# A third quarter of x turned by VectorE's blocks, where TensorE transposed it before

## The chip, the core and the metric

The kernel runs on one core of one Trainium2 chip. The time is the device time of one execution in microseconds (us); of several runs the median is given. The engines are TensorE (PE in the profile, PEld its weight loads), VectorE (DVE), ScalarE (ACT), GpSimd (POOL) and SyncE (SP, here the queue that issues most DMAs).

## What is computed

One step of a decoder layer for 256 prompt tokens and 8 x 4 sample tokens, 288 in all, with 2048 features, in float32. Only the first lines matter here: the residual x meets one wide input projection, and everything else follows from that.

```python
def hybrid_layer(x, ..., w_in, ...):
    proj = x @ w_in
    split_points = np.cumsum(SPLITS)[:-1].tolist()
    gB, gC, h, q, k, v, z, b_logit, a_logit, m_a, m_b = jnp.split(proj, split_points, axis=-1)
...
    merged = jax.nn.sigmoid(m_a) * y_a + jax.nn.sigmoid(m_b) * y_b
    x = layer_norm(ALPHA * x + merged @ w_o, ln1_g, ln1_b)
    hid = jnp.square(jax.nn.relu(x @ w_up))
    x = layer_norm(ALPHA * x + hid @ w_down, ln2_g, ln2_b)
```

## The kernel before

The whole kernel is a list of some 500 *blocks* (512 KB of weights each) that TensorE works through in order, one `matmuls(i)` after the other. For float32 accuracy each weight tile `raw` is split into a rounded part `hi` (ScalarE, `split_hi`, line 187) and a rest `lo = raw - hi` (VectorE, `split_lo`, through `tt`, line 142); the activations are split the same way into `xh` and `xl`. A block is 24 matmuls of 288 columns in four groups of six: twice xh and xl against hi (line 219), then twice xh against lo (line 221). The 288 columns are 256 prompt tokens and 32 sample tokens, so the first xl matmul of a block needs both.

The features of x must lie on the partitions: x has to be turned. This is done at the start, beside the first blocks, by quarters of 512 features (4 of the 16 tiles in `xh` and `xl`). The order of the blocks is set by hand: blocks 0 to 3 are wide ones, which use the first two quarters (0 and 1 the first, 2 and 3 the second), blocks 4 and 5 use quarter 2, blocks 6 and 7 quarter 3. All engines run their instructions in the order in which the code issues them; nothing reorders them.

There are two ways to turn a quarter.

- By TensorE (quarters 0, 1 and 2): `x_steps` gives eight transposes of 128x128 into PSUM (line 957), ScalarE casts the result to `xh` (line 963), VectorE subtracts it to get `xl` (line 142). These steps are put between the matmuls of the block before by the list `fill`: after the second pair of lo matmuls one step is taken from it. For quarter 2 this is `x_fill(2)`, put in at `i == 3`.
- By VectorE (quarter 3 alone): `x_turn` turns 32x32 blocks in one instruction, `xr[3]` to `xtb` (line 980); `x_moves` then moves sixteen pieces of 32 partitions by 256 columns to their places in `xm` (line 987), ten on GpSimd and six on ScalarE; `x_last` casts `xm` to `xh` on ScalarE (line 992) and subtracts on VectorE, in two halves.

The sample's 32 columns of each quarter are always transposed by TensorE (`x_sample`, line 941), cast by ScalarE (line 946) and subtracted by VectorE. The loop that sets the order around the change, in the kernel before:

```python
matmuls(i)
if i == 4:
    x_last()
if i < 6:
    for u, step in {0: ((1, 2),), 1: ((2, 1), (3, KB))}.get(i, ((i + 2, KB),)):
        split_hi(u, step)
        split_lo(u, step)
if i == 2:
    x_turn()
    x_moves(gps.tensor_copy, range(10))
if i == 3:
    x_moves(act.copy, range(10, 16))
```

In the program's names `hi`, `lo` and `raw` carry running numbers: before, `lo_262` is block 2's, `lo_269` block 3's, `lo_299` block 4's, `lo_358` block 5's, `lo_398` block 6's; with the change these are `lo_264`, `lo_280`, `lo_310`, `lo_367`, `lo_403`.

Of the kernel before, what the change touches and what calls it, by code (L numbers as in the profile page):

```python
# [9 lines left out]
F32 = mybir.dt.float32  # L10
# [6 lines left out]
P = 128  # L17
# [88 lines left out]
def hybrid_kernel(ctx: ExitStack, tc: tile.TileContext, A):  # L106
# [3 lines left out]
    def pool(name, bufs=1, **kw):  # L110
        return ctx.enter_context(tc.tile_pool(name=name, bufs=bufs, **kw))
# [10 lines left out]
    def nm(s):  # L122
        counter[0] += 1
        return f"{s}{counter[0]}"

    def gtile():
        n = nm("g")
        return gp.tile([P, 512], F32, tag="g", name=n)
# [9 lines left out]
    act, dve, pe, gps, sp = nc.scalar, nc.vector, nc.tensor, nc.gpsimd, nc.sync  # L138


    def tt(out, a, b, op):
        dve.tensor_tensor(out=out, in0=a, in1=b, op=op)  # L142
# [18 lines left out]
    fill = []  # L161

    def at(i, f):
        due.setdefault(i, []).append(f)
# [18 lines left out]
    def split_hi(i, step=KB):  # L183
        if i < len(blocks):
            his[i] = wp.tile([P, KB, GW], F32R, tag="hi", name=nm("hi"))
            for k in range(0, KB, step):
                act.copy(his[i][:, k:k + step], raw[i][:, k:k + step])  # L187

    def split_lo(i, step=KB):
        if i < len(blocks):  # L190
            los[i] = wp.tile([P, KB, GW], F32R, tag="lo", name=nm("lo"))
            r = raw[i] if blocks[i][0].get("by_token") else raw.pop(i)
            for k in range(0, KB, step):
                tt(los[i][:, k:k + step], r[:, k:k + step], his[i][:, k:k + step], SUB)
# [682 lines left out]
    tx = tx_cm.__enter__()  # L877
# [9 lines left out]
    xr = [tx.tile([P, 2, 512], F32, name=f"xr{i}") for i in range(4)]  # L887
# [1 line left out]
    xpr = A["x_prompt"][0].rearrange("(b p) f -> p b f", p=P)  # L889
    xsr = A["x_sample"].rearrange("b t (c j p) -> c (b t) j p", j=4, p=P)  # L890

    xtb, xm = (tx.tile([P, 1024], F32, name=n) for n in ("xtb", "xm"))
    hwr = tx.tile([112, 768], F32, name="hwr")
    har = tx.tile([76, 256], F32, name="har")
    lnr = tx.tile([33, P], F32, name="lnr")
# [43 lines left out]
    def x_sample(i):  # L939
        g = gtile()  # L940
        pe.transpose(g[:, 0:P], xs4[:, i * P:(i + 1) * P], ident)
        gv = g[:, 0:P].rearrange("p (t j) -> p j t", j=4)
        xv, xw = (u[:, 4 * i:4 * i + 4, NP_:NT] for u in (xh, xl))

        def out(copy=act.copy):
            copy(xv, gv)  # L946
            tt(xw, gv, xv, SUB)
        return out
# [21 lines left out]
    def x_fill(i):  # L970
        def step(u):
            def f():
                turns, out = x_steps(i)[u]()
                for g in turns + out:
                    g()
            return f
        return step(0), lambda: x_sample(i)(), step(1)

    def x_turn():
        dve.transpose(out=xtb, in_=xr[3].rearrange("p b c -> p (b c)"))  # L980

    def x_moves(copy, ns):
        src = xtb.rearrange("p (b k j r) -> p j b k r", b=2, k=4, j=4)
        dst = xm.rearrange("p (k b w r) -> p w b k r", k=4, b=2, w=4)
        for n in ns:
            w, j = n // 4, n % 4
            copy(dst[32 * j:32 * j + 32, w], src[32 * w:32 * w + 32, j])

    def x_last():
        for k in (0, 2):  # L990
            ks, xv = slice(12 + k, 14 + k), xm.rearrange("p (k t) -> p k t", k=4)[:, k:k + 2]
            act.copy(xh[:, ks, 0:NP_], xv)
            tt(xl[:, ks, 0:NP_], xv, xh[:, ks, 0:NP_], SUB)

# [577 lines left out]
    def states_out(t0, t1, npr, n, tag, prompt, sample):  # L1572
        st = gd["pool"].tile([P, t1 - t0, 32], F32, tag=tag, name=nm("st"))
        for t in range(t0, t1, 8):
            dve.transpose(out=st[:, t - t0:t - t0 + 8].rearrange("p t c -> p (t c)"),
                          in_=stBA[:, t:t + 8].rearrange("p t c -> p (t c)"))
        for i in range(4):
            for dst, r0, r1 in ((prompt, 0, npr), (sample.rearrange("b j c -> (b j) c"), npr, n)):
                gps.dma_start(dst.rearrange("r (t i c) -> i r t c", i=4, c=32)[i], st[32 * i + r0:32 * i + r1])
# [18 lines left out]
    t, h0, l0 = raw.pop(0), his[0], los[0]  # L1598
# [21 lines left out]
    idle = lambda: None  # L1620
# [23 lines left out]
    for i in range(len(blocks)):  # L1644
        cur[0] = i
        ahead = AHEAD if i > 9 else 2
        if i == 10:
            split_hi(i + 2)
            split_lo(i + 2)
        if i > 5:  # L1650
            split_hi(i + ahead)
        if i in (1, 3):
            a_, s_, b_ = x_fill(i // 2 + 1)
            fill.extend([idle, a_, s_, b_])
        if i == 5:
            fill.extend([idle, idle, lambda: x_sample(3)()])
        if i == 6:
            fill.extend([idle, idle, idle, idle, hist_tiles, hist_tiles2])
        if i == 7:
            tx_cm.__exit__(None, None, None)  # L1660
            gcm = tc.tile_pool(name="gdn", bufs=1)
            gpool = gcm.__enter__()
            gd["pool"] = gpool
            gd["w1"] = [gpool.tile([P, 640], F32, tag=f"w1{u}", name=f"w1{u}") for u in range(2)]
            for w in gd["w1"]:
                gps.memset(w[:, 0:3], 0.0)
            gps.memset(stBA, 0.0)
            for G in range(2):
                gd["kq", G] = gpool.tile([P, 4, 4, 2, 64], F32, tag="kq", name=f"kq{G}", bufs=2)
                gd["kqs", G] = gpool.tile([P, 2, 4, 8, 4], F32, tag="kqs", name=f"kqs{G}", bufs=2)  # L1670
                gd["v", G] = gpool.tile([P, 2, 4, 2, 64], F32, tag="vf", name=f"vf{G}")
                gd["vs", G] = gpool.tile([P, 4, 8, 4], F32, tag="vfs", name=f"vfs{G}")
        if i > 7 and sgen:
            if i == mark["merge"]:
                for _ in sgen:
                    pass
                sgen = None
            else:
                next(sgen, None)
                if aux and next(aux[0], aux) is aux:  # L1680
                    aux.pop(0)
            if i == mark["z"] + 4:
                states_out(24, 32, 2, 18, "vf", A["new_conv_a_prompt"][0, 0], A["new_conv_a_sample"][0])
            if i == mark["conv"] + 1:
                gd["ao"] = ap_.tile([P, 2, H, NT], F32, tag="ao", name="ao")
        late = i >= mark["end"] - 1
        if i > 5 and not late:
            split_lo(i + ahead)
        for f in due.pop(i, ()):
            f()  # L1690
        if late:
            split_lo(i + ahead)
        if i == mark["merge"]:
            gcm.__exit__(None, None, None)
            p3 = pool("p3")
            ph["pool"] = p3
            r1 = p3.tile([P, KT, NT], F32R, tag="R1", name="ahl")
            r4 = p3.tile([P, KT, NX], F32R, tag="R4", name="ohl")
            ph["mg"] = p3.tile([P, KT, NX], F32, tag="R3", name="mg")[:, :, 0:NT]

            def halves(key, r, src):
                for q in range(2):
                    s = slice(4 * q, 4 * q + 4)
                    s8 = slice(8 + 4 * q, 12 + 4 * q)
                    act.copy(r[:, s, 0:NT], src[:, s, :])
                    tt(r[:, s8, 0:NT], src[:, s, :], r[:, s, 0:NT], SUB)
                ph[key + "h"], ph[key + "l"] = r[:, 0:8, :], r[:, 8:16, :]

            halves("a", r1, gd["ao"][:, 0])
            at(i + 9, lambda: halves("o", r4, gd["ao"][:, 1]))  # L1710
        if i == mark["down3"]:
            tail_tiles()
        if i == mark["down3"] - 60:
            tail_consts()
        if i == mark["end"] - 3:
            sample_sum()
        if i == mark["end"] - 1:
            sample_products()
        matmuls(i)
        if i == 4:  # L1720
            x_last()
        if i < 6:
            for u, step in {0: ((1, 2),), 1: ((2, 1), (3, KB))}.get(i, ((i + 2, KB),)):
                split_hi(u, step)
                split_lo(u, step)
        if i == 2:
            x_turn()
            x_moves(gps.tensor_copy, range(10))
        if i == 3:
            x_moves(act.copy, range(10, 16))  # L1730
        if i == 10:
            load(i + 6)
        load(i + ahead + 4)
        if 4 <= i < 8:
            rest[i - 4]()
# [33 lines left out]
```

## Time and profile before

| | us |
|---|---|
| median of 3 runs | 1661.09 (1659.30 to 1661.68) |
| the profiled execution | 1658.95 |
| its span, first to last instruction | 1656.8 |
| busy in the span: TensorE | 1648.6 |
| VectorE | 981.2 |
| ScalarE | 785.8 |
| GpSimd | 138.8 |

The profile is one execution; its times run from the span's start. Between span and time lie 2.15 us. Matmuls are pipelined: one of 288 columns lasts 0.29 us from start to end, and the next begins 0.13 us after it. So the starts are what to read, not the busy time. In a row, the name left of the arrow is written and those right of it are read, buffer numbers are left out (`lo<-raw,hi`), x and a number at the end count the instructions in the row, and what stands in brackets is idle time before the row and what ended it.

### The profile page before, as it was taken

The numbers are of one execution on the slowest core, as the hardware profiler recorded it, in microseconds if no ns is written. First come the engines' busy times: TensorE is split into PE (matmuls) and PEld (weight loads), VectorE is DVE, ScalarE is ACT, GpSimd is POOL, SyncE is SP. The second block draws the span as 40 slices with busy tenths as digits, with TensorE's granted clock in tenths as the row PEclk, the third lists the DMA queues.
The fourth block names the chain that finished last, engine by engine and source line by source line (L and its number), as shares of the span: only waits on it lengthen the run. The fifth ranks groups of instructions, "written<-read, shape, count | busy, mean of one in ns | idle before, by whom it ended". The sixth has DMA issues, their size and how long they took to land.

```text
span 1656.8 us, 31402 instructions
## 1 busy us (share of the span) xinstructions
PE 1648.6 (100%) x13130; PEld 1634.0 (99%) x13130; DVE 981.2 (59%) x1299; ACT 785.8 (47%) x1231; POOL 138.8 (8%) x273
## 2 busy tenths in 40 slices
PE   9999999999999999999999999999999999999998
PEld 8999999999999999999999999999999999999997
DVE  6798678767544444457776666444444444444466
ACT  6786756448533333334444455443334433344354
POOL 1142216133000000000000000000000000000011
PEclk9999999999999999999999999999999999999999
DMA  8555457545555555554565555555555555555552
GB/s 272 176 169 172 135 173 203 184 130 175 185 170 165 166 165 165 166 166 157 167 217 164 166 166 166 166 166 166 165 166 166 166 166 165 166 166 166 180 162 100
DMA packets 273236, 280.42 MB, mean 169 GB/s; under 512 B 13727, under 2 KB 267220, under 8 KB 272832
## 3 DMA queue, kind: packets, MB, share of 16 engines
q1 hardware_dynamic: 269334, 266.33, 51.2%
q0 software_dynamic: 3616, 12.02, 2.6%
q8 instruction: 103, 1.69, 0.4%
q14 instruction: 39, 0.32, 0.1%
q10 hardware_dynamic: 144, 0.07, 0.0%
HBM read 270.88 MB, written 7.48 MB: 168 GB/s over the span
## 4 chain that ended last, share of the span: by engine, by line
PE 98%; DVE 1%; ACT 1%; DMA 0%; issue 0%; SPq 0%; ACTq 0%
PE acc L219 62%; PE acc L221 31%; PE acc L739 1%; PE g L1328 0%; PE g L1500 0%; PE g L1520 0%; PE g L1523 0%; DMA xr<-in_x_prompt_dram 0%; PE g L1319 0%; PE g L1220 0%; PE g L1478 0%; DVE lo L142 0%; PE g L1512 0%; DVE w L145 0%; DVE Y L145 0%
## 5 line engine op out<-in xcount | busy, mean ns | idle before, releaser
L142 DVE TENSOR_TENSOR lo<-raw,hi 128x1024 fp32r<-128x1024 f32 (+1 forms) x503 | 607.3, 1210 | 576.7 <-ACT hi L187 573.7
L187 ACT CAST hi<-raw 128x1024 fp32r<-128x1024 f32 (+1 forms) x499 | 519.1, 1043 | 729.5 <-PE acc L219 657.0
L219 PE MATMUL acc<-xh,hi 128*128 128x288 f32 x1408 | 397.9, 298 | 0.3 <-ACT xh L946 0.2
L219 PE MATMUL acc<-xl,hi 128*128 128x288 f32 x1408 | 394.2, 295 | 0.0
L221 PE MATMUL acc<-xh,lo 128*128 128x288 f32 x1408 | 302.6, 296 | 0.2 <-DVE lo L142 0.2
L219 PE MATMUL acc<-dl,hi 128*128 128x288 f32 (+1 forms) x1024 | 287.7, 295 | 0.0
L219 PE MATMUL acc<-dh,hi 128*128 128x288 f32 (+1 forms) x1024 | 287.4, 295 | 0.0
L219 PE MATMUL acc<-hl,hi 128*128 128x288 f32 x992 | 277.8, 295 | 0.0
L219 PE MATMUL acc<-hh,hi 128*128 128x288 f32 x992 | 277.4, 294 | 0.0
L219 PEld LDWEIGHTS acc<-xh,hi 128*128 128x128 f32 x1408 | 264.4, 188 | 3.1 <-issue 1.6
L219 PEld LDWEIGHTS acc<-xl,hi 128*128 128x128 f32 x1408 | 264.2, 188 | 1.1 <-DVE xl L142 0.3
L221 PEld LDWEIGHTS acc<-xh,lo 128*128 128x128 f32 x1408 | 226.0, 188 | 0.7 <-DVE lo L142 0.6
L221 PE MATMUL acc<-dh,lo 128*128 128x288 f32 (+1 forms) x1024 | 219.8, 296 | 0.0
L221 PE MATMUL acc<-hh,lo 128*128 128x288 f32 x992 | 213.2, 296 | 0.0
L219 PEld LDWEIGHTS acc<-dh,hi 128*128 128x128 f32 x1024 | 193.3, 189 | 0.0
L219 PEld LDWEIGHTS acc<-dl,hi 128*128 128x128 f32 x1024 | 192.8, 188 | 0.0
L219 PEld LDWEIGHTS acc<-hh,hi 128*128 128x128 f32 x992 | 186.4, 188 | 0.4 <-issue 0.4
L219 PEld LDWEIGHTS acc<-hl,hi 128*128 128x128 f32 x992 | 186.1, 188 | 0.0
L221 PEld LDWEIGHTS acc<-dh,lo 128*128 128x128 f32 x1024 | 164.5, 188 | 0.0
L221 PEld LDWEIGHTS acc<-hh,lo 128*128 128x128 f32 x992 | 159.0, 188 | 0.0
L219 PE MATMUL acc<-mh,hi 128*128 128x288 f32 x256 | 71.9, 297 | 0.0
L219 PE MATMUL acc<-ml,hi 128*128 128x288 f32 x256 | 71.7, 295 | 0.0
(423 smaller groups left out, 1489.1 us busy)
## 6 DMA issues: line engine op xcount, KB each, us to landing
raw<-in_w_in_dram SPq DMA_DIRECT2D x175, 512.0 KB, 3.5
raw<-in_w_up_dram SPq DMA_DIRECT2D x128, 512.0 KB, 3.6
raw<-in_w_down_dram SPq DMA_DIRECT2D x128, 512.0 KB, 3.6
raw<-in_w_o_dram SPq DMA_DIRECT2D x32, 512.0 KB, 3.7
raw<-in_w_a_out_dram SPq DMA_DIRECT2D x16, 512.0 KB, 3.6
raw<-in_w_b_out_dram SPq DMA_DIRECT2D x16, 512.0 KB, 3.6
S<-in_state_gdn_dram POOLq DMA_DIRECT2D x8, 512.0 KB, 5.5
out_dram<-S POOLq DMA_DIRECT2D x8, 512.0 KB, 4.7
```

The source lines that it names most:

```text
L142: dve.tensor_tensor(out=out, in0=a, in1=b, op=op)
L187: act.copy(his[i][:, k:k + step], raw[i][:, k:k + step])
L219: pe.matmul(o, h[:, k, c], x, start=st and x is xh_, stop=False)
L221: pe.matmul(o, l[:, k, c], xh_, start=False, stop=en)
L739: pe.matmul(out, x[:, kk, c], w[:, k, :], start=False, stop=stop)
```

## The change

Quarter 2 is now turned as quarter 3 is: `x_turn`, `x_moves` and `x_last` take the quarter as an argument, with an `xtb` and an `xm` for each of the two. For quarter 2 GpSimd moves eight pieces and ScalarE eight; for quarter 3 still ten and six. TensorE loses the eight prompt transposes of quarter 2; the sample's transpose stays in block 3. In the loop the turn of quarter 2 is issued after `split_hi(3)` and ahead of `split_lo(3)`, the turn of quarter 3 stays behind `split_lo(4)`, `x_last(2)` comes at the end of `i == 2`, and `x_last(3)` moves behind `split_hi(6)` and `split_lo(6)`.

```diff
--- before.py
+++ after.py
@@ -889,7 +889,7 @@
     xpr = A["x_prompt"][0].rearrange("(b p) f -> p b f", p=P)
     xsr = A["x_sample"].rearrange("b t (c j p) -> c (b t) j p", j=4, p=P)
 
-    xtb, xm = (tx.tile([P, 1024], F32, name=n) for n in ("xtb", "xm"))
+    xtb, xm = ({c: tx.tile([P, 1024], F32, name=f"{n}{c}") for c in (2, 3)} for n in ("xtb", "xm"))
     hwr = tx.tile([112, 768], F32, name="hwr")
     har = tx.tile([76, 256], F32, name="har")
     lnr = tx.tile([33, P], F32, name="lnr")
@@ -976,19 +976,19 @@
             return f
         return step(0), lambda: x_sample(i)(), step(1)
 
-    def x_turn():
-        dve.transpose(out=xtb, in_=xr[3].rearrange("p b c -> p (b c)"))
-
-    def x_moves(copy, ns):
-        src = xtb.rearrange("p (b k j r) -> p j b k r", b=2, k=4, j=4)
-        dst = xm.rearrange("p (k b w r) -> p w b k r", k=4, b=2, w=4)
+    def x_turn(i):
+        dve.transpose(out=xtb[i], in_=xr[i].rearrange("p b c -> p (b c)"))
+
+    def x_moves(i, copy, ns):
+        src = xtb[i].rearrange("p (b k j r) -> p j b k r", b=2, k=4, j=4)
+        dst = xm[i].rearrange("p (k b w r) -> p w b k r", k=4, b=2, w=4)
         for n in ns:
             w, j = n // 4, n % 4
             copy(dst[32 * j:32 * j + 32, w], src[32 * w:32 * w + 32, j])
 
-    def x_last():
+    def x_last(i):
         for k in (0, 2):
-            ks, xv = slice(12 + k, 14 + k), xm.rearrange("p (k t) -> p k t", k=4)[:, k:k + 2]
+            ks, xv = slice(4 * i + k, 4 * i + 2 + k), xm[i].rearrange("p (k t) -> p k t", k=4)[:, k:k + 2]
             act.copy(xh[:, ks, 0:NP_], xv)
             tt(xl[:, ks, 0:NP_], xv, xh[:, ks, 0:NP_], SUB)
 
@@ -1649,11 +1649,11 @@
             split_lo(i + 2)
         if i > 5:
             split_hi(i + ahead)
-        if i in (1, 3):
+        if i == 1:
             a_, s_, b_ = x_fill(i // 2 + 1)
             fill.extend([idle, a_, s_, b_])
-        if i == 5:
-            fill.extend([idle, idle, lambda: x_sample(3)()])
+        if i in (3, 5):
+            fill.extend([idle, idle, lambda i=i: x_sample(i // 2 + 1)()])
         if i == 6:
             fill.extend([idle, idle, idle, idle, hist_tiles, hist_tiles2])
         if i == 7:
@@ -1717,17 +1717,22 @@
         if i == mark["end"] - 1:
             sample_products()
         matmuls(i)
-        if i == 4:
-            x_last()
         if i < 6:
             for u, step in {0: ((1, 2),), 1: ((2, 1), (3, KB))}.get(i, ((i + 2, KB),)):
                 split_hi(u, step)
+                if u == 3:
+                    x_turn(2)
+                    x_moves(2, gps.tensor_copy, range(8))
                 split_lo(u, step)
         if i == 2:
-            x_turn()
-            x_moves(gps.tensor_copy, range(10))
+            x_moves(2, act.copy, range(8, 16))
+            x_turn(3)
+            x_moves(3, gps.tensor_copy, range(10))
+            x_last(2)
         if i == 3:
-            x_moves(act.copy, range(10, 16))
+            x_moves(3, act.copy, range(10, 16))
+        if i == 4:
+            x_last(3)
         if i == 10:
             load(i + 6)
         load(i + ahead + 4)
```

On VectorE, from block 2's lo to the sample of quarter 3, before:

```order
L142 TENSOR_TENSOR lo_262<-raw_124,hi_257 128x256 x4
L142 TENSOR_TENSOR lo_269<-raw_126,hi_267 128x1024
L142 TENSOR_TENSOR lo_299<-raw_150,hi_297 128x1024
L980 STREAM_TRANSPOSE xtb<-xr_106 128x1024
L142 TENSOR_TENSOR xl<-g_320,xh 128x2x256
L142 TENSOR_TENSOR xl<-g_332,xh 128x4x32
L142 TENSOR_TENSOR xl<-g_337,xh 128x2x256
L142 TENSOR_TENSOR lo_358<-raw_154,hi_356 128x1024
L142 TENSOR_TENSOR xl<-xm,xh 128x2x256 x2
L142 TENSOR_TENSOR lo_398<-raw_213,hi_396 128x1024
L142 TENSOR_TENSOR xl<-g_414,xh 128x4x32
```

and with the change:

```order
L142 TENSOR_TENSOR lo_264<-raw_126,hi_259 128x256 x4
L980 STREAM_TRANSPOSE xtb_108<-xr_105 128x1024
L142 TENSOR_TENSOR lo_280<-raw_128,hi_269 128x1024
L142 TENSOR_TENSOR lo_310<-raw_152,hi_308 128x1024
L980 STREAM_TRANSPOSE xtb_109<-xr_106 128x1024
L142 TENSOR_TENSOR xl<-xm_110,xh 128x2x256 x2
L142 TENSOR_TENSOR xl<-g_348,xh 128x4x32
L142 TENSOR_TENSOR lo_367<-raw_156,hi_365 128x1024
L142 TENSOR_TENSOR lo_403<-raw_215,hi_401 128x1024
L142 TENSOR_TENSOR xl<-xm_111,xh 128x2x256 x2
L142 TENSOR_TENSOR xl<-g_423,xh 128x4x32
```

The transpose of quarter 2 (`xtb_108`) now stands ahead of block 3's lo. The two xl of quarter 2 read `xm_110` and have the sample's behind them, and those of quarter 3 stand behind block 6's lo and no longer ahead of it.

On ScalarE, from the hi of block 3 to the sample of quarter 3, before (`hi_267`, `hi_297`, `hi_356` and `hi_396` are those of blocks 3 to 6):

```order
L187 CAST hi_267<-raw_126 128x1024
L187 CAST hi_297<-raw_150 128x1024
L963 CAST xh<-g_320 128x2x256
L946 CAST xh<-g_332 128x4x32
L963 CAST xh<-g_337 128x2x256
L187 CAST hi_356<-raw_154 128x1024
L987 COPY xm<-xtb 32x2x4x32 x6
L992 CAST xh<-xm 128x2x256 x2
L187 CAST hi_396<-raw_213 128x1024
L946 CAST xh<-g_414 128x4x32
```

and with the change (`hi_269`, `hi_308`, `hi_365` and `hi_401`):

```order
L187 CAST hi_269<-raw_128 128x1024
L187 CAST hi_308<-raw_152 128x1024
L987 COPY xm_110<-xtb_108 32x2x4x32 x8
L992 CAST xh<-xm_110 128x2x256 x2
L946 CAST xh<-g_348 128x4x32
L187 CAST hi_365<-raw_156 128x1024
L987 COPY xm_111<-xtb_109 32x2x4x32 x6
L187 CAST hi_401<-raw_215 128x1024
L992 CAST xh<-xm_111 128x2x256 x2
L946 CAST xh<-g_423 128x4x32
```

Eight copies stand behind block 4's hi, then both evacuations of quarter 2, which wait for GpSimd's part of `xm_110`, then the sample's, and only then block 5's hi. The evacuation of quarter 3 comes behind block 6's hi.

On GpSimd the eight copies of quarter 2 stand ahead of the ten of quarter 3, with nothing between. The order on SP is the same as before.

## Rows read from the trace of the kernel before

**Rows 1.** The page's section 4: shares of the chain that ended last, by engine.

```profile
PE 98%; DVE 1%; ACT 1%; DMA 0%; issue 0%; SPq 0%; ACTq 0%
```

**Rows 2.** TensorE's timeline, blocks 3 to 6: start us, us, instruction.

```profile
17.79 0.29 PE L219 MATMUL acc<-xh,hi 128*128 128x288 f32 x1
...
18.58 0.60 PE L957 MATMUL g<-cf,xr 128*128 128x128 f32 x4
18.94 0.38 PE L219 MATMUL acc<-xh,hi 128*128 128x288 f32 x1
...
21.96 0.29 PE L219 MATMUL acc<-xh,hi 128*128 128x288 f32 x1
22.09 0.29 PE L219 MATMUL acc<-xl,hi 128*128 128x288 f32 x1
...
28.44 0.29 PE L219 MATMUL acc<-xh,hi 128*128 128x288 f32 x1
28.59 0.40 PE L219 MATMUL acc<-xl,hi 128*128 128x288 f32 x1
28.83 0.30 PE L219 MATMUL acc<-xh,hi 128*128 128x288 f32 x1
```

**Rows 3.** The timeline of VectorE, narrow windows around blocks 2 to 6.

```profile
15.10 0.76 DVE L142 TENSOR_TENSOR lo<-raw,hi 128x256 fp32r<-128x256 f32 x2
...
17.30 1.23 DVE L142 TENSOR_TENSOR lo<-raw,hi 128x1024 fp32r<-128x1024 f32 x1
...
18.44 1.24 DVE L980 STREAM_TRANSPOSE xtb<-xr 128x1024 f32<-128x1024 f32 x1
...
25.63 1.29 DVE L142 TENSOR_TENSOR xl<-xm,xh 128x512 fp32r<-128x512 f32 x2 [2.25 <-ACT xh L992]
...
28.25 0.28 DVE L142 TENSOR_TENSOR xl<-g,xh 128x128 fp32r<-128x128 f32 x1
```

**Rows 4.** The timeline of ScalarE around blocks 4 to 6.

```profile
16.22 1.05 ACT L187 CAST hi<-raw 128x1024 fp32r<-128x1024 f32 x1 [0.26 <-DMA raw<-in_w_in_dram]
...
22.11 2.48 ACT L987 COPY xm<-xtb 32x256 f32<-32x256 f32 x6
24.98 1.14 ACT L992 CAST xh<-xm 128x512 fp32r<-128x512 f32 x2 [0.39 <-POOL xm L987]
```

**Rows 5.** The timelines of GpSimd and VectorE around the copies of quarter 3.

```profile
19.75 5.20 POOL L987 COPY xm<-xtb 32x256 f32<-32x256 f32 x10 [18.33 <-DVE xtb L980]
...
22.35 1.29 POOL L987 COPY xm<-xtb 32x256 f32<-32x256 f32 x1
...
22.12 1.27 DVE L142 TENSOR_TENSOR lo<-raw,hi 128x1024 fp32r<-128x1024 f32 x1 [0.25 <-ACT hi L187]
```

**Rows 6.** The same two engines later, by narrow windows, where copies meet other work.

```profile
247.26 1.30 POOL L1562 COPY ao<-v 32x256 f32<-32x256 f32 x1
...
246.88 1.42 DVE L142 TENSOR_TENSOR lo<-raw,hi 128x1024 fp32r<-128x1024 f32 x1
...
84.83 0.39 POOL L1179 COPY kdec<-S 32x256 f32<-32x256 f32 x1
...
84.78 0.70 DVE L1162 STREAM_TRANSPOSE S<-kq 128x512 f32<-128x512 f32 x1
```

**Rows 7.** The timeline of SP and the tile view of xr: issue and landing.

```profile
6.30 0.47 SPq L920 DMA_DIRECT2D xr<-in_x_prompt_dram  x1
...
DMA to landing us min/median/max: 2.3/8.1/8.6
```

**Rows 8.** TensorE at start and end; in the window row PEclk stands before DMA.

```profile
0.99 2.31 PE L884 MATMUL g<-warm 128*128 128x512 bf16 x5 [0.99 <-DVE warm L879]
...
7.20 0.43 PE L219 MATMUL acc<-xl,hi 128*128 128x288 f32 x2
...
1650.96 0.96 PE L801 MATMUL g<-g 6*128 6x512 f32 x3 [0.34 <-ACT g L798]
...
1653.00:1654.00 1.00, 0.00 (x0) 0.00 (x0) 0.00 (x0) 0.00 (x0) 0.00 (x0) 0.56 1.01 371
```

## The prediction

> **What bounds the kernel now.** Read the chain of waits that ended last first: 98% of it is TensorE's [rows 1]. So the kernel loses time only where TensorE stands still, and gains only where TensorE has less to do or stands still less. The second view is TensorE's order of time around the change. The wide blocks 0 to 3 use the first half of x, blocks 4 and 5 the third quarter, blocks 6 and 7 the fourth. In block 3 (from 17.79) the reader sees two groups of four transposes, the first at 18.58; block 4 follows at 21.96 without a gap, its second matmul, the first that reads xl, at 22.09. Only at 28.59 is something late: the second matmul of block 6 starts 0.15 us after the first and the third 0.24 us after that, where 0.13 is the pace [rows 2]. The releaser is the sample part of xl for quarter 3, which ends at 28.53 [rows 3]. So the first xl matmul of a block needs the whole chain for its quarter: both halves of xh and xl and the 32 sample columns, whose VectorE instruction stands last. That is the chain to follow for block 4 once quarter 2 is built in the new way.
>
> The third thing to read is GpSimd. It moves 32x256 pieces of the turned quarter at some 0.43 us each (the first starts at 19.75; without the long one the rest fit that pace), but one took 1.29 us: it started at 22.35, while VectorE's lo of 128x1024 ran from 22.12 to 23.39, and ended 0.25 us after it [rows 5]. Later the same is seen in a back-to-back pair: a copy that starts at 247.26 beside a lo from 246.88 to 248.30 ends at 248.56. Beside VectorE's transpose of 84.78 to 85.48 a copy took the plain 0.39 [rows 6]. I read: a copy that starts during a VectorE subtraction of two SBUF tensors comes out about 0.26 us after that subtraction, one copy per subtraction; a block transpose does not hold it.
>
> **Part by part.** *Removed:* eight TensorE transposes, four from 18.58 to 18.94 [rows 2], so 0.36 us for four and 0.72 for both groups at least. At most it is 1.0: block 3 takes 21.96 - 17.79 = 4.17 us where its 24 matmuls at 0.13 make 3.15, and the sample's transpose, which stays, is in that too. I take 0.9, eight ninths of the 1.0, since that one is a ninth of the transposes. Block 3 would then end, and block 4 could start, at 21.96 - 0.9 = 21.06. Also removed are ScalarE's and VectorE's two evacuations from PSUM; two of the same size from SBUF replace them.
>
> *Added:* on VectorE one transpose of 1.24 us [rows 3], before the lo of block 3; on GpSimd eight copies before the ten it had; on ScalarE eight copies before the evacuations of quarter 2. *No DMA is added or moved:* SP's order is the same, and xr of quarter 2, issued at 6.30, has landed by 6.30 + 8.6 = 14.9 even at the longest landing [rows 7].
>
> The chain of block 4, step by step.
> 1. VectorE's last small lo ends at 15.10 + 0.76 = 15.86, and a follower starts some 0.09 before its forerunner's end (17.30 + 1.23 against 18.44) [rows 3]: the transpose runs 15.77 to 17.01. Behind it the lo of block 3 runs 16.92 to 18.15. TensorE wants that at 17.79 + 4 x 0.13 = 18.3 [rows 2], so it is covered by 0.15 us; if that cover goes, TensorE waits for the excess, but the wait at block 4 swallows it. The lo of block 4 runs 18.06 to 19.29, the second transpose 19.20 to 20.44.
> 2. GpSimd starts at 17.07, inside the lo of block 3: first copy out at 18.15 + 0.26 = 18.41; the second starts inside the lo of block 4 and is out at 19.29 + 0.26 = 19.55. Six at 0.43 follow: 22.15.
> 3. ScalarE: the hi of block 4 ends at 16.22 + 1.05 = 17.27; eight copies at 2.48 / 6 = 0.41 end at 20.6 [rows 4]. They hide behind GpSimd. Then it waits, with hi of block 5 queued behind.
> 4. xh from 22.19, two in 1.14; xl starts 0.65 behind xh (25.63 against 24.98), so 22.84, two in 1.29 to 24.13; the sample's xl of 0.28 ends at 24.32 [rows 3, 4]. TensorE starts 0.06 after that: 24.38.
>
> Against 22.09 this is **+2.3 us**. TensorE stands from 21.06 to 24.38 with one matmul (the first, on xh) in between: the 0.9 is spent, and 2.3 more.
>
> *What is late next.* After its wait ScalarE casts the sample's columns and hi of block 5 (1.05 each hi, so to some 24.5), moves six pieces (to 27.0) and makes hi of block 6 (to 28.0); block 5 only starts at 27.5, so its hi and its lo (24.5 to 25.7) are in time. GpSimd starts quarter 3 at 22.2; the two xl and the lo of block 5 hold three of its ten copies, and it ends at 27.7, before ScalarE is free. Then xh from 28.0, lo of block 6 to 29.2, xl to 30.4, sample to 30.6, TensorE 30.7. Block 6's second matmul comes at 28.57 + 2.3 = 30.87: in time by some 0.2 us, and the 0.12 us that is lost there now [rows 2] is saved. The two later loads that wait for these lo are issued at most 2.3 us later, as much as TensorE itself. From block 7 on the kernel is as before, shifted.
>
> **The sum:** +2.3 - 0.1 = +2.2 us. On the profiled execution (1658.95 us) that is 1661.15; its time lies 2.14 below the median of the three runs, 1661.09, so for a median I forecast **1663.3 us**. A measurement of this kernel can tell about 0.2%, 3.3 us, from no change: the forecast is "no change" with a small loss in it.
>
> *Bounds of the unknown.* No row shows GpSimd's copies beside two lo and a transpose in this very place. From below: no copy is held, and GpSimd ends at 17.07 + 8 x 0.43 = 20.5, ScalarE's 20.6 decides, everything comes 1.56 earlier: +0.6. From above: the transpose holds a copy as well, so the third comes out at 20.44 + 0.26 = 20.70, and the eighth at 22.86: +2.9. I take +2.2, since the rows of a copy beside a subtraction and beside a transpose [rows 5, 6] are the same operations at the same sizes. The Trainium skill speaks for the upper end: "GPSIMD Engine Reference", section 1 Specifications, has GpSimd in contention with VectorE instructions that have two SBUF inputs or run in a 2-port mode, and "VectorE: DVE Perf Modes", What auto-detection actually checks, lets an instruction with one source and destination in SBUF go into a 2-port mode; by the two of them the transpose would hold GpSimd too, and the sum be +2.9 and not the +2.2 by the rows. The trace does not agree for the transpose: 1024 columns take 1.24 us, as long as a subtraction of two tensors [rows 3], and the copy beside one is not held [rows 6].
>
> **Rivals.**
> *The clock falls in the gap (slower).* TensorE would idle 3.3 us but for one matmul. At the end of the kernel, after its last three sparse matmuls (to 1651.92), the granted clock is 0.56 in 1653 to 1654 [rows 8]: it fell some 1.2 us after the last of them (0.56 is about an eighth of that microsecond at 1 and the rest at 0.5). If it falls to 1.2 GHz here, the next matmuls take twice as long until it rises. At the start five warm-up matmuls of 512 columns take 2.31 us, 0.46 each, the lower level, and at 7.20 two of 288 columns fit 0.43 with their latency, as everywhere later: the upper [rows 8]. So a low stretch lasts between 2.3 us and 6.2 (0.99 to 7.20), and costs half of it, 1.2 to 3.1; I take 1.8, nearer the lower end, because after the gap work is dense at once: +4.0, 1665.1 us. It decides if a gap of that length, with one matmul in it, is enough for a fall as the end's was. The Trainium skill ("TensorE: Matmul & The Clock Gate", What's actually happening) also has it that the throttled state is the default and activity releases it; this case's end agrees. Against: the gap is short, with dense work on both sides. 0.22.
>
> *The transpose holds GpSimd:* +2.9, 1664.0 us, worked out above, which is the pages' rule as a mechanism of this kernel. 0.08.
>
> *GpSimd is not held:* +0.6, 1661.7 us. Against it stands the 1.29. 0.12.
>
> *The chain is hidden after all* and the removed transposes count in full: -0.9 - 0.1 = -1.0, 1660.1 us. For it: ScalarE now has idle time ahead of quarter 3's evacuation. Against: even with unheld copies the chain ends at 22.8, 1.7 us after block 4 could start. 0.05.
>
> **How the numbers follow.** The forecast gets 0.53. The three runs before span 1659.30 to 1661.68, so a median can stand a microsecond off. Slower by over 0.2%: most of the clock case, 0.18, and a rest of 0.07 of the forecast and the held transpose: 0.25. Faster by over 0.2% would need more than the removed transposes can give: 0.02. Same: 0.73. The range goes from the hidden chain (1660.1) to the clock case (1665.1), with a little of that microsecond at either end: 1659.8 to 1666.3.
>
> **What would show it.** Right: TensorE's idle time before block 4 at about 21.1, released by xh (sample) between 23.3 and 23.7 and by xl (sample) at 24.3; two GpSimd copies of over 1 us among the first eight, ending near 18.4 and 19.6; xh of quarter 2 released by GpSimd at 22.2; no wait at block 6. Wrong: block 4 starting at 21.1 without a wait; a third long copy beside the second transpose; a granted clock under 1 behind the gap; or a stall at block 3 or block 6 that this sum has at nothing.

## The result, and the profile after

| | before | changed |
|---|---|---|
| median us (lowest to highest) | 1659.87 (1658.87 to 1661.70), 17 runs | 1663.96 (1662.95 to 1667.23), 17 runs |
| the profiled execution, us | 1658.95 | 1663.26 |
| its span, us | 1656.8 | 1661.1 |

The ratio is 1.0026, with a 95% interval of 1.0019 to 1.0034: slower by 4.1 us, a quarter of a per cent. The range held it; the likeliest case (+2.2) did not come, the rival of +4.0 did. The page of the changed kernel, busy time of each engine and the chain's shares:

```profile
PE 1649.6 (99%) x13122; PEld 1634.5 (98%) x13122; DVE 982.6 (59%) x1300; ACT 789.2 (48%) x1239; POOL 144.6 (9%) x281
...
PE 97%; DVE 1%; ACT 1%; POOL 0%; DMA 0%; issue 0%; SPq 0%; ACTq 0%
```

TensorE's share of the chain is one point lower than in [rows 1], and GpSimd now appears in it, at 0%. TensorE's timeline, the lines that answer to [rows 2] (start us, us, instruction; in brackets idle time and what ended it):

```profile
17.91 0.29 PE L219 MATMUL acc<-xh,hi 128*128 128x288 f32 x1
...
20.93 0.42 PE L221 MATMUL acc<-xh,lo 128*128 128x288 f32 x2
23.84 0.40 PE L219 MATMUL acc<-xh,hi 128*128 128x288 f32 x1 [2.49 <-ACT xh L946]
24.94 0.61 PE L219 MATMUL acc<-xl,hi 128*128 128x288 f32 x1 [0.70 <-DVE xl L142]
...
26.78 0.44 PE L219 MATMUL acc<-xh,hi 128*128 128x288 f32 x1
27.02 0.44 PE L219 MATMUL acc<-xl,hi 128*128 128x288 f32 x1
...
28.14 0.29 PE L219 MATMUL acc<-xh,hi 128*128 128x288 f32 x1
28.27 0.29 PE L219 MATMUL acc<-xl,hi 128*128 128x288 f32 x1
...
29.47 0.29 PE L219 MATMUL acc<-xh,hi 128*128 128x288 f32 x1
...
32.77 0.29 PE L219 MATMUL acc<-xh,hi 128*128 128x288 f32 x1
32.90 0.29 PE L219 MATMUL acc<-xl,hi 128*128 128x288 f32 x1
```

Three things are to be seen. Block 3's last matmul starts at 21.06 and TensorE then stands, but for one matmul at 23.84, until 24.94. Behind that a matmul starts 0.24 us after the one before it (26.78, 27.02), and only from 28.14 on 0.13 again. And block 6 has lost its wait: its second matmul starts 0.13 after the first. Starts in this trace lie 0.12 us later than in [rows 2] already at block 3 (17.91 against 17.79), so all that follows is measured from block 3's first matmul. The 0.24 is the clock, in a table by stretches of 2 us (busy time of each engine; PEclk is the number before the last two):

```profile
22.00:24.00 2.00, 0.16 (x1) 0.16 (x1) 0.86 (x2) 1.51 (x4) 1.82 (x5) 1.00 0.69 192
24.00:26.00 2.00, 1.30 (x5) 1.09 (x6) 2.00 (x3) 1.94 (x5) 1.92 (x3) 0.65 1.07 373
26.00:28.00 2.00, 2.00 (x11) 2.00 (x10) 0.02 (x1) 1.95 (x4) 1.83 (x5) 0.50 0.70 217
28.00:30.00 2.00, 2.00 (x17) 2.00 (x17) 1.67 (x2) 1.44 (x3) 0.41 (x2) 0.99 0.46 160
```

The granted clock is 1.00 up to 24, 0.50 from 26 to 28 (the level of 1.2 GHz) and back at 0.99 behind that. 0.65 in 24 to 26 is 0.6 us at 1 and 1.4 at 0.5; so it was low for some 3.4 us, beginning near 24.6, when TensorE had stood since 21.35 but for one matmul, and 0.3 us before it started again.

The whole loss can be read from starts. Block 4's second matmul comes 24.94 - 17.91 = 7.03 us after block 3's first, where it was 22.09 - 17.79 = 4.30: **+2.73**. From there to block 5 it is 29.47 - 24.94 = 4.53, before 25.15 - 22.09 = 3.06: **+1.47**. The wait at block 6 gives **-0.1** back. Together 4.11 at block 10; the two profiled executions lie 4.31 apart, the medians 4.09.

The chain that feeds block 4, first GpSimd, then VectorE, then ScalarE:

```profile
17.20 1.30 POOL L987 COPY xm<-xtb 32x256 f32<-32x256 f32 x1 [15.78 <-DVE xtb L980]
...
18.54 1.30 POOL L987 COPY xm<-xtb 32x256 f32<-32x256 f32 x1
...
19.88 0.84 POOL L987 COPY xm<-xtb 32x256 f32<-32x256 f32 x2
...
21.62 0.83 POOL L987 COPY xm<-xtb 32x256 f32<-32x256 f32 x2
```

```profile
15.89 1.24 DVE L980 STREAM_TRANSPOSE xtb<-xr 128x1024 f32<-128x1024 f32 x1
...
17.06 1.18 DVE L142 TENSOR_TENSOR lo<-raw,hi 128x1024 fp32r<-128x1024 f32 x1
...
18.16 1.42 DVE L142 TENSOR_TENSOR lo<-raw,hi 128x1024 fp32r<-128x1024 f32 x1
...
19.50 1.23 DVE L980 STREAM_TRANSPOSE xtb<-xr 128x1024 f32<-128x1024 f32 x1
23.14 1.54 DVE L142 TENSOR_TENSOR xl<-xm,xh 128x512 fp32r<-128x512 f32 x2 [2.41 <-ACT xh L992]
24.61 0.28 DVE L142 TENSOR_TENSOR xl<-g,xh 128x128 fp32r<-128x128 f32 x1
```

```profile
17.26 3.31 ACT L987 COPY xm<-xtb 32x256 f32<-32x256 f32 x8
22.49 1.14 ACT L992 CAST xh<-xm 128x512 fp32r<-128x512 f32 x2 [1.92 <-POOL xm L987]
```

GpSimd's first two copies take 1.30 each: the first starts inside the lo of block 3 and ends at 18.50, 0.26 after it; the second starts inside the lo of block 4 and ends 0.26 after that. The pair from 19.88 runs beside the second transpose and takes 0.84. ScalarE's eight are done at 20.57, and it waits 1.92 for GpSimd's eighth, which ends at 22.45.

### The profile page after: what moved, and what is told of

The parts are those of the page before. It is cut to its first block, busy times and chain, and to the rows that moved or that the text cites. A ratio compares the mean times of both kernels' runs of the same rounds, so it can differ in the third digit from the quotient of the medians.

```text
span 1661.1 us, 31401 instructions
## 1 busy us (share of the span) xinstructions
PE 1649.6 (99%) x13122; PEld 1634.5 (98%) x13122; DVE 982.6 (59%) x1300; ACT 789.2 (48%) x1239; POOL 144.6 (9%) x281
## 4 chain that ended last, share of the span: by engine, by line
PE 97%; DVE 1%; ACT 1%; POOL 0%; DMA 0%; issue 0%; SPq 0%; ACTq 0%
PE acc L219 62%; PE acc L221 31%; PE acc L739 1%; PE g L1328 0%; PE g L1500 0%; PE g L1520 0%; PE g L1523 0%; DVE lo L142 0%; POOL xm L987 0%; DMA xr<-in_x_prompt_dram 0%; PE g L1319 0%; PE g L1220 0%; PE g L1478 0%; PE g L1512 0%; DVE w L145 0%
```

## The experiments

**Theory:** the chain over GpSimd, held by two subtractions, costs 2.7 us net of the transposes; a fall of the clock that the gap brings about costs the other 1.4. **Rivals:** the 0.24 pace comes with the order of the work, not with the gap; it is not GpSimd's hold but the shared copying, or the sample's place at the chain's end, that makes the delay; the transposes are worth more or less than 0.9. E1 to E4 ran on one chip, E5 to E7 and the repetition on another, each timed against the kernel before on its chip. Each time in the table is a difference of two starts in that run's own trace; the fourth column says by how much more than before block 10 comes behind block 3's first matmul.

| run | block 4's second matmul after block 3's first | from there to block 6's second | block 10 against before | ratio, 95% |
|---|---|---|---|---|
| before | 4.30 | 6.50 | 0 | |
| changed | 7.03 | 7.96 | +4.11 | 1.0026 (1.0019 to 1.0034) |
| changed, again | 7.04 | 8.11 | +4.26 | one run |
| E1, TensorE kept busy | 7.02 | 6.59 | +2.73 | 1.0020 (1.0011 to 1.0029) |
| E2, sample first | 5.91 | 8.10 | +3.13 | 1.0015 (1.0006 to 1.0024) |
| E3, no transposes | 3.41 | 8.05 | +0.67 | 1.0004 (0.9995 to 1.0014) |
| E4, turned later | 7.69 | 8.11 | +4.92 | 1.0032 (1.0020 to 1.0045) |
| E5, 6 and 10 copies | 5.14 | 7.06 | +1.40 | 1.0006 (0.9997 to 1.0015) |
| E6, three engines | 5.18 | 8.10 | +2.50 | 1.0013 (1.0004 to 1.0022) |
| E7, none turned | 3.42 | 6.50 | -0.96 | 0.9996 (0.9987 to 1.0005) |

**E1: TensorE kept busy in the gap.** Eleven matmuls whose results nobody reads, ahead of block 4.

```diff
+        if i == 4:
+            wg = gtile()
+            for _ in range(11):
+                pe.matmul(wg.rearrange("p (u c) -> p u c", u=4), warm, bmid(warm, 4), start=True, stop=True)
         matmuls(i)
```

> The changed kernel, with eleven matmuls of 128x512 on the warm-up tile (results unused) put between blocks 3 and 4, where TensorE waits. They take 11 x 0.22 = 2.4 us at the upper clock level and end at about 23.6, before xh is there (23.8), so they delay nothing. If the loss has two parts, a wait of 2.8 us at block 4 and a clock that falls behind it (1.3 to 1.6 us), the granted clock stays at 1.00 to the end, block 4's second matmul stays at 24.9, and the kernel is 1.3 to 1.6 us faster than the changed one: 1662.4 to 1662.7 on a median of 1663.96, 1.0016 of the kernel before. Rival, the clock has nothing to do with the idle time (it falls for another reason, or its rows mean nothing): the clock falls as before and the time stays at 1664 (1.0026).

Measured: the granted clock stays up; block 4 is as late as in the changed kernel, but runs at full pace. TensorE's timeline, and two stretches of the same view as above:

```profile
21.29 2.55 PE L1722 MATMUL g<-warm 128*128 128x512 bf16 x11
...
25.02 0.40 PE L219 MATMUL acc<-xl,hi 128*128 128x288 f32 x1 [0.70 <-DVE xl L142]
25.26 0.30 PE L219 MATMUL acc<-xh,hi 128*128 128x288 f32 x1
...
28.18 0.29 PE L219 MATMUL acc<-xh,hi 128*128 128x288 f32 x1
```

```profile
24.00:26.00 2.00, 1.30 (x8) 1.09 (x9) 2.00 (x3) 1.95 (x4) 1.92 (x3) 1.00 1.07 360
26.00:28.00 2.00, 2.00 (x17) 2.00 (x16) 0.10 (x1) 1.94 (x5) 1.83 (x5) 1.00 0.69 179
```

From the second matmul to block 5 it is 28.18 - 25.02 = 3.16 us in place of 4.53: the low clock cost 1.37. (The 0.1 over the 3.06 of the kernel before is the lone second matmul, whose successor starts 0.24 behind it.) The stall is the same, 7.02. So the two losses are separate, and the slow pace comes from the gap. The times alone hardly show it: 1.0020 with an interval that still takes in 1.0026.

**E2: the sample ahead of the chain.** The sample's transpose goes into block 2 and its xh and xl ahead of the prompt's, so that the chain ends with xl.

```diff
+    xs_two = []
...
-        if i in (3, 5):
-            fill.extend([idle, idle, lambda i=i: x_sample(i // 2 + 1)()])
+        if i == 2:
+            fill.extend([idle, idle, lambda: xs_two.append(x_sample(2))])
+        if i == 5:
+            fill.extend([idle, idle, lambda: x_sample(3)()])
...
+            xs_two.pop()()
             x_last(2)
```

> The changed kernel, with the sample of quarter 2 transposed in block 2 and evacuated ahead of the two halves of quarter 2. If the first xl matmul of block 4 waits for the sample's xl because it stands last, it now waits for the first half alone: it starts at about 23.9 and not at 24.94, the wait is 1.0 us shorter, and TensorE's idle time before block 4 falls from 2.5 to some 1.8 us. Then the kernel is 1.0 us faster than the changed one if the clock still falls, and some 2.5 faster if it does not (1661.5 to 1663.0). Rival, the first matmul needs both halves whatever the order: the second xl ends at about 24.7, and the gain is 0.2 us.

Measured: as expected, block 4's second matmul comes 1.12 us earlier (5.91 for 7.03). The gap is shorter, and in the profiled execution the clock falls all the same. VectorE's timeline, the first of the two xl, then TensorE's, the second matmul, and the stretch behind it:

```profile
23.84 0.74 DVE L142 TENSOR_TENSOR xl<-xm,xh 128x512 fp32r<-128x512 f32 x1 [2.04 <-ACT xh L992]
```

```profile
24.64 0.40 PE L219 MATMUL acc<-xl,hi 128*128 128x288 f32 x1 [0.38 <-DVE xl L142]
```

```profile
26.00:28.00 2.00, 2.00 (x11) 2.00 (x10) 0.72 (x1) 1.93 (x6) 1.88 (x4) 0.50 0.24 47
```

The second matmul starts 0.06 us after the first xl ends (24.58), while the second xl runs until 25.38: it needs the first half and the sample alone. In the changed kernel the sample's xl, which it also needs, stands behind both halves, so it waits for all three. The sample's place is thus 1.1 of the 2.7 us; the other 1.6 us are the chain ahead of it.

**E3: what the transposes are worth.** In the kernel before, quarter 2 is cast and subtracted from SBUF unturned; quarter 3 stays as it was.

```diff
+    def x_unturned(i):
+        for k in range(2):
+            ks, xv = slice(4 * i + 2 * k, 4 * i + 2 * k + 2), xr[i][:, k].rearrange("p (k t) -> p k t", k=2)
+            act.copy(xh[:, ks, 0:NP_], xv)
+            tt(xl[:, ks, 0:NP_], xv, xh[:, ks, 0:NP_], SUB)
...
-        if i in (1, 3):
+        if i == 1:
...
+        if i == 3:
+            fill.extend([idle, idle, lambda: (x_sample(2)(), x_unturned(2))])
```

> The kernel before, without the eight transposes of quarter 2: its xh and xl are cast and subtracted from the rows of x as they lie, unturned, so that the outputs are those of another x; the same casts and subtractions are made, from SBUF and not from PSUM, and at once. This is what the change could have gained at most, with the wait gone. By my step (0.72 to 1.0 us, 0.9 taken) block 4's first matmul starts at 21.0 to 21.2 against 21.96 and the kernel gains 0.7 to 1.0 us (0.9995 of before). Rival, the transposes fill a wait that stands there anyway (on the lo of block 3 or 4, or on hi): then block 4 starts at about 21.9 and nothing is gained.

Measured: block 4 follows block 3's start by 22.54 - 19.26 = 3.28 us in place of 4.17, so 0.89 is saved, as priced. But the time does not fall. TensorE's timeline at block 6, and GpSimd's ten copies of quarter 3:

```profile
29.42 0.40 PE L219 MATMUL acc<-xh,hi 128*128 128x288 f32 x1 [0.23 <-ACT xh L946]
30.72 0.40 PE L219 MATMUL acc<-xl,hi 128*128 128x288 f32 x1 [0.90 <-DVE xl L142]
```

```profile
21.04 6.04 POOL L993 COPY xm<-xtb 32x256 f32<-32x256 f32 x10 [19.63 <-DVE xtb L986]
```

The ten took 5.20 in [rows 5]; here two xl of SBUF and one lo hold them, 6.04. Block 6's second matmul comes 11.46 us after block 3's first, before 10.80. What the missing transposes gave is taken back there, and more. The expectation of a gain in time was a miss: it left out that quarter 3's chain ends last at block 6 already in the kernel before.

**E4: turned later.** The first transpose and its moves go behind the lo of block 4, so that no copy of quarter 2 meets a subtraction.

```diff
-                if u == 3:
-                    x_turn(2)
-                    x_moves(2, gps.tensor_copy, range(8))
...
         if i == 2:
+            x_turn(2)
+            x_moves(2, gps.tensor_copy, range(8))
```

> The changed kernel, with the turn of quarter 2 behind the lo of blocks 3 and 4 and not ahead of them, so that no subtraction runs beside GpSimd's eight copies, but a block transpose does. If VectorE's subtractions hold GpSimd and its transpose does not, all eight copies take 0.39 to 0.40 us; they start at about 19.7 and end at about 23.1, 0.6 us later than the 22.46 of the changed kernel although they start 2.5 us later. The kernel is then 0.6 us slower than the changed one. Rival, the long copies come from something else, such as ScalarE's copies from the same tile beside them: then two of the eight are long again, they end at about 24.9, and the kernel is some 2.4 us slower than the changed one.

Measured: no copy is held. GpSimd's timeline, three places among the eight of quarter 2:

```profile
19.98 0.39 POOL L987 COPY xm<-xtb 32x256 f32<-32x256 f32 x1 [18.57 <-DVE xtb L980]
...
20.41 0.83 POOL L987 COPY xm<-xtb 32x256 f32<-32x256 f32 x2
...
22.58 0.83 POOL L987 COPY xm<-xtb 32x256 f32<-32x256 f32 x2
```

ScalarE copies beside them as in the changed kernel, and the second transpose runs until 21.04: neither costs GpSimd anything. What holds a copy is the subtraction of two SBUF tensors. As a cure it does not help, since the first copy starts 2.5 us later (19.98 - 18.20 = 1.78 behind block 3's start, against -0.71) and the 1.8 us that the eight save do not make up for that: block 4's second matmul comes 0.66 later than in the changed kernel.

**E5: the moves balanced.** E2, with six pieces on GpSimd and ten on ScalarE.

```diff
-                    x_moves(2, gps.tensor_copy, range(8))
+                    x_moves(2, gps.tensor_copy, range(6))
...
-            x_moves(2, act.copy, range(8, 16))
+            x_moves(2, act.copy, range(6, 16))
```

> As the kernel with the sample first, and of quarter 2's sixteen pieces GpSimd moves six and ScalarE ten (eight and eight before). GpSimd's two held copies and four plain ones end 0.87 us earlier, at 21.6, and ScalarE's ten at 21.4, both counted with block 3 starting at 17.9. So block 4's second matmul starts 5.0 us after block 3's first (before the change 4.3, changed 7.0, sample first 5.9). TensorE waits about 1.0 and then 0.8 us, and I expect the clock to stay up. If the chain through GpSimd sets block 4, that leaves +0.75 us there. Quarter 3's chain is then late at block 6, by some 0.8 us, because TensorE comes to it sooner: in all 1.0 to 1.6 us slower than before (1.0006 to 1.0010). Rival, ScalarE or VectorE sets block 4: no change against the sample-first kernel at block 4.

Measured: TensorE's timeline at blocks 4 and 6, and the clock behind the gap:

```profile
22.54 0.40 PE L219 MATMUL acc<-xh,hi 128*128 128x288 f32 x1 [1.07 <-ACT xh L992]
23.26 0.40 PE L219 MATMUL acc<-xl,hi 128*128 128x288 f32 x1 [0.33 <-DVE xl L142]
...
29.71 0.29 PE L219 MATMUL acc<-xh,hi 128*128 128x288 f32 x1
30.32 0.40 PE L219 MATMUL acc<-xl,hi 128*128 128x288 f32 x1 [0.32 <-DVE xl L142]
```

```profile
24.00:26.00 2.00, 2.00 (x17) 2.00 (x16) 1.34 (x2) 1.95 (x5) 1.92 (x3) 1.00 0.97 332
```

Block 4's second matmul is 5.14 after block 3 (0.8 later than before), the clock stays at 1.00, and 0.6 us is lost at block 6. Most of the change's loss is gone, and what is left is still no gain over the kernel before.

**E6: VectorE moves pieces too.** E2, with four pieces on GpSimd, nine on ScalarE and three on VectorE ahead of the second transpose.

```diff
-                    x_moves(2, gps.tensor_copy, range(8))
+                    x_moves(2, gps.tensor_copy, range(4))
...
-            x_moves(2, act.copy, range(8, 16))
+            x_moves(2, act.copy, range(4, 13))
+            x_moves(2, dve.tensor_copy, range(13, 16))
             x_turn(3)
```

> As above, with four pieces of quarter 2 on GpSimd, nine on ScalarE and three on VectorE, between the lo of block 4 and the turn of quarter 3. Pieces ready at about 21.0 (with block 3 at 17.9); the first xl waits for the later second turn, so block 4's second matmul starts 4.5 to 4.8 us after block 3's first. Then the loss at block 4 is 0.2 to 0.5 us against the kernel before, and that at block 6 (quarter 3, whose turn comes 0.9 us later) about 0.8: in all 0.9 to 1.3 us slower than before (1.0005 to 1.0008). If the loss at block 4 were all that there is, it would be 0.3 us.

Measured: a miss, +2.50. The timelines of TensorE, VectorE and GpSimd:

```profile
23.09 0.40 PE L219 MATMUL acc<-xl,hi 128*128 128x288 f32 x1 [0.78 <-DVE xl L142]
...
31.19 0.40 PE L219 MATMUL acc<-xl,hi 128*128 128x288 f32 x1 [0.45 <-DVE xl L142]
```

```profile
20.79 1.25 DVE L980 STREAM_TRANSPOSE xtb<-xr 128x1024 f32<-128x1024 f32 x1
...
22.14 1.70 DVE L142 TENSOR_TENSOR xl<-xm,xh 128x512 fp32r<-128x512 f32 x2
```

```profile
27.23 1.29 POOL L987 COPY xm<-xtb 32x256 f32<-32x256 f32 x1
```

The pieces on VectorE push the second transpose to 20.79, and xl of quarter 2, in order behind it, starts only at 22.14 and takes 1.70 instead of 1.29. Quarter 3's copies start later too, so that one more of them meets a lo (27.23), and block 6 waits.

**E7: the most that there is to gain.** E3 with quarter 3 unturned as well: no transposes for the prompt behind quarter 1, no blocks, no moves.

```diff
         if i == 4:
-            x_last()
+            x_unturned(3)
...
-        if i == 2:
-            x_turn()
-            x_moves(gps.tensor_copy, range(10))
-        if i == 3:
-            x_moves(act.copy, range(10, 16))
```

> The kernel before without the eight transposes, with quarters 2 and 3 both taken unturned (outputs are those of another x), so that neither chain can be late. If the eight transposes cost 0.9 us and the loss in the kernel without them came from quarter 3's chain at block 6, block 4 starts 3.3 us after block 3 (4.17 before), block 6 has no wait, and the kernel is 0.9 to 1.0 us faster than before (0.9994). Rival, TensorE's later blocks wait for something else as soon as it is ahead (weights on their way, hi): then a wait of the same size stands at block 5 to 9 and nothing is gained.

Measured: no wait is left at blocks 4 to 6; block 10 comes 0.96 earlier, which is the 0.9 of the transposes and the 0.1 at block 6. In the times that is 0.9996, not to be told from 1. With the rest of the kernel as it is, all that an arrangement of the turns of quarters 2 and 3 could win is about 1 us in 1660.

**The changed kernel once more**, unchanged, for one profile.

> The changed kernel unchanged, profiled once more. If the wait brings the clock down whenever it comes, the granted clock falls again behind the wait, for the same 3.4 us, and block 4's second matmul starts 7.0 us after block 3's first. If the fall was an accident of one execution, the clock stays at 1.00 this time.

Measured: the same stall, and the clock falls again. TensorE's timeline, and the clock:

```profile
26.55 0.40 PE L219 MATMUL acc<-xl,hi 128*128 128x288 f32 x1 [0.70 <-DVE xl L142]
```

```profile
26.00:28.00 2.00, 1.45 (x9) 1.46 (x10) 1.63 (x3) 1.94 (x5) 1.92 (x3) 0.89 0.25 89
28.00:30.00 2.00, 2.00 (x11) 2.00 (x10) 0.06 (x1) 1.86 (x4) 1.83 (x5) 0.50 0.54 124
```

It falls later here: 0.89 in 26 to 28 is 0.44 us at half clock, so the fall comes near 27.56, and TensorE had by then worked at full pace for 1.0 us. In E2 it came 0.8 us after the second matmul (0.87 in 24 to 26). So the fall follows the gap, but not at a fixed time, and the price depends on where it lies: from the second matmul to block 5 it is 31.23 - 26.55 = 4.68 us here and the same in E2, 1.52 more than in E1, against 1.37 in the first profile.

That it falls in most executions, if not all, can be read from the mean granted clock that each run reports: 0.997 or 0.998 in all 17 runs of the changed kernel, 0.999 in 53 of the 55 runs of the kernel before on the two chips, 0.999 in 9 of 11 of E1. E2 has 0.998 in 8 of its 11 runs and 0.999 in three, E5 and E6 0.999 or 1.0 in 10 and 9 of 11. Some 3.4 us at half clock are 0.001 of 1661.

## Why the prediction was right and wrong

**The step that failed** is the rival *the clock falls in the gap*, which got 0.22 and came true. Its price was near: 1.8 forecast, 1.37 measured (E1; 1.52 in the second profile). The argument against it, "the gap is short, with dense work on both sides", had no row behind it, while the only row on the question, that of the kernel's end [rows 8], showed a fall some 1.2 us after the last matmul. The Trainium skill ("TensorE: Matmul & The Clock Gate", What's actually happening) has the throttled state as the default, which activity releases. E1's 1.00 against the 0.50 of the changed kernel agrees.

**The term of the sum that was mis-sized** is the stall: "+2.3 us" for block 4's second matmul, measured +2.73. The chain came as described, but VectorE's subtractions were taken at their undisturbed length. The hold works both ways: a subtraction that starts while a copy still runs is late in its turn. The lo of block 3 started ahead of the first copy (17.06 against 17.20), held it and took 1.18; the lo of block 4 started at 18.16, while that copy ran until 18.50, and took 1.42 and not 1.23 (+0.2, through GpSimd's second copy). The two xl took 1.54 among GpSimd's copies of quarter 3, not 1.29 (+0.25). The row was there: the lo of 246.88 in [rows 6] took 1.42, and was read for the copy's end alone.

**A reading that was too strong:** that a block's first xl matmul needs both halves of its quarter. E2 shows that it needs the first half and the sample; it waits for the second because the sample's xl stands behind it, and that order, which the prediction took as given, is 1.1 us of the stall. The sum for this kernel, in which the sample does stand last, is not touched by it.

Point by point otherwise:

- *The removed transposes, 0.9:* right; 0.89 in E3, and E7's 0.96 with block 6's wait.
- *Two copies held, by 0.26 behind each subtraction; the transpose doesn't hold:* right; 1.30 twice, then 0.84 for two beside the transpose, and E4 shows it from the other side. The rivals with the held transpose (+2.9) and with no hold (+0.6) are out. Of the rule of the Trainium skill weighed there ("GPSIMD Engine Reference", section 1 Specifications), contention with VectorE instructions that have two SBUF inputs or run in a 2-port mode, the trace shows the first part at these subtractions. For this transpose it shows no hold; no run here tells in which mode the transpose runs.
- *ScalarE's eight copies hidden, ending at 20.6:* right, 20.57; xh followed GpSimd's last copy at 22.49 (22.19 forecast).
- *Block 3's lo covered by 0.15:* right; no wait there.
- *Block 6 in time by 0.2, its 0.12 saved:* right; the low clock, which delays block 6 by 1.4, gave it more room, but E1 has no wait there either. One step of it was off: GpSimd's ten copies of quarter 3 end at 28.46, after ScalarE is free (28.30), and not before. E3, E5 and E6, in which block 4 starts earlier, lose 0.6 to 1.6 us from block 4 to block 6 (7.06 to 8.10 against 6.50 before): quarter 3's chain is the next bound, as the prediction's "late next" had it.
- *The chances:* the ratio 1.0026 lies over the bound of 0.2%, on the side that got 0.25; its interval reaches just under it. 4.0 = 2.2 + 1.8 met 4.1 = 2.7 + 1.4: two errors of 0.4 to 0.5 that cancel, so the rival's total is no proof of its parts. That 1663.3 lies within 0.7 us of the measured 1663.96 is luck as well: it was built on the 1661.09 of three runs, where 17 runs give 1659.87 before, and as a loss 2.2 was forecast and 4.1 came.

What stays open: which property of a gap decides whether the clock falls. It fell at idle times of 2.49 and 0.70 us around the lone matmul (changed, twice), 1.79 and 0.38 (E2), 3.2 and 0.7 (E4); it stayed at 1.07 and 0.33 (E5), at 0.66 and 0.78 (E6), at 0.23 and 0.90 (E3, block 6), and with E1's filling. No run varied the gap alone, and none shows what sets the moment of the fall.

## What to carry to other kernels

Where work is taken off an engine that is never idle and given to others, ask first what its next input then waits for: 0.9 us less of TensorE's work was paid for with a chain over three engines that put the next block 2.7 us back. A stall on TensorE can have a second price behind it, the clock (1.4 to 1.5 us here, nothing behind the shorter stalls of E3, E5 and E6); read the granted clock after any pause that the trace already has before calling a new gap harmless. And where two engines contend, price both: the row that shows the one held also shows the other slowed.

## What was not expected of the hardware

- In these traces, where a subtraction of two SBUF tensors and a GpSimd copy meet, the one that starts first goes on and the other is late. A subtraction that starts ahead of the copy keeps its time (1.18 us at 17.06); one that starts while a copy runs is slowed: 1.42 for 1.23 us (128x1024) and 1.54 for 1.29 (two of 128x512); in E6 1.70.
- A copy that meets a subtraction of half the size is held for less: 0.76 us beside an xl of 128x512 (changed kernel, at 23.38), against 1.30 beside a lo.
- TensorE reaches its full pace at a different time in different executions. The changed kernel's two profiles, the same pair of matmuls of block 0:

```profile
7.31 0.42 PE L219 MATMUL acc<-xl,hi 128*128 128x288 f32 x2
```

```profile
7.81 0.68 PE L219 MATMUL acc<-xl,hi 128*128 128x288 f32 x2
```

  Two matmuls take 0.42 in the first and 0.68 in the second, which reaches block 3 at 19.51 instead of 17.91. That is 1.6 us of difference between executions of one kernel, about as much as the low clock behind the gap costs, and the reason why traces are compared here from block 3 on. The granted clock shows nothing of it: it reads 1.00 in every microsecond of the start, so the low pace there, and the low stretch that the prediction took from [rows 8], rest on durations alone.
